# Another token order in the branch gates' products, with another block size in each of eight stages

## The chip, the cores and the metric

The kernel runs on one core of a Trainium2 chip. The metric is the time of one execution on the device in microseconds, as the median of several runs. TensorE multiplies and writes to the accumulator memory PSUM; ScalarE (ACT) and VectorE (DVE) work on tiles in SBUF and PSUM; SyncE (SP) and GpSimd (POOL) issue the transfers.

## The reference

One layer of a decoder trunk on 256 tokens of width 1024, in float32, every projection without a batch:

```python
proj = jnp.einsum("bsd,dn->bsn", x, w_in) + b_in
q_m, k_m, v_m, o_m, i_m, f_m, q_b, k_b, v_b, g_a, g_b = _split_cols(proj, SPLIT_SIZES)
# an mLSTM branch (4 heads x 256) gives y_a, an attention branch (8 heads x 128) gives y_b
merged = (jax.nn.sigmoid(g_a) * jnp.einsum("bsw,wd->bsd", y_a, w_branch_a)
          + jax.nn.sigmoid(g_b) * jnp.einsum("bsw,wd->bsd", y_b, w_branch_b))
mix = jnp.einsum("bsd,de->bse", merged, w_out)
x = layer_norm(ALPHA * x + mix, ln1_g, ln1_b)
# then a gated MLP with a short convolution, and a second layer norm
```

The change touches `g_a` and `g_b`, the two branch gates: each is a product of all 256 tokens with a 1024 x 1024 block of `w_in`, and a bias.

## The kernel before

All weights come from HBM as a stream of 89 chunks of 128 partitions x 2048 words (1 MB each), in the order that `chunk_order` gives. One chunk is one stage of the program. A chunk of a projection holds 256 output columns for all 1024 inputs, as 8 tiles (`KT`) of 128 inputs.

Every product is made of three float32r matmuls, so that nearly float32's precision is kept: each operand is split into a rounded high part (ScalarE, L93) and the remainder (VectorE, L94), and `mm3` (L126) adds high x high (L129), high weights x low tokens (L130) and low weights x high tokens (L131) into one PSUM tile.

In `mm_feat` (L133) the weights are the stationary operand, 128 columns of them, and the tokens are the moving one: all 256 columns of one input tile, `xh[:, k, :]`, 1024 contiguous bytes in each partition. One stage has two halves of 128 outputs (`j`), each with 8 input tiles and 3 matmuls: 48 matmuls of 256 columns. In `mm_tok` (L147) the roles are the other way round. While one matmul streams its columns, TensorE loads the next one's weights (the rows named PEld).

After four chunks for the output gate come four groups with eight stages each: `qm, qb, km, kb, vm, vb, ga, gb`. Two of these, `ga` and `gb`, are the branch gates (`step_gate`, L514). So there are eight gate stages, two in each group, each for 256 of the 1024 gate columns. A gate's PSUM tile is evacuated one stage later by two ScalarE instructions with the bias, which write the gate to `sg["ga"]` or `sg["gb"]` in SBUF. The gates are read much later, in the stages `wa` and `wb`, where the branches are merged.

The order of the work is written out by hand, stage by stage: in stage s the evacuation of stage s-1 and the split of chunk s+2 are issued, the load of chunk s+5, then the stage's matmuls, then what small products of the attention and the mLSTM fall into it (`side_pe`). The gate stages in groups 0 to 2 have such small products before and behind them: `psl` (attention logits, 256 columns and a float32 product of 128) and `psn` (258 columns). Three PSUM buffers (tag "mm") go round among the big stages.

Two functions set where in a buffer the weights of a chunk start: `shift` (L61) gives a number of columns by the kind of chunk, and `odd` (L1148) gives a few chunks 8 columns more or less in a part of the buffer and sets an input tile first.

Of the kernel before, what the change touches and what calls it, by code (L numbers as in the profile page):

```python
# [13 lines left out]
AF = mybir.ActivationFunctionType  # L14
# [4 lines left out]
P = 128  # L19
# [53 lines left out]
class Kernel:  # L73
# [26 lines left out]
    def split_parts(self, s):  # L100
        if s >= len(self.order) or s in self.w:
            return []
        raw = self.raw.pop(s)
        if s in self.extra:
            wh, wl = self.extra.pop(s)
            a = 8
        else:
            wh = self.stream.tile([P, WCOLS], F32R, tag="wh", name=f"wh{s}", bufs=3)
            wl = self.stream.tile([P, WCOLS], F32R, tag="wl", name=f"wl{s}", bufs=3)
            a = shift(*self.order[s])  # L110

        e, z, n, _ = odd(*self.order[s])
        wh, wl = (t[:, a - e:a + 2048 + z] for t in (wh, wl))
        edges = sorted({0, 256 if e else 0, 2048 if self.order[s][0] == "up" and self.order[s][1] >= 6 else 1024, 2048 - n, 2048})
        cuts = [(*(t[:, self.col(s, b):self.col(s, b) + d - b] for t in (wh, wl)), raw[:, b:d])
                for b, d in zip(edges, edges[1:])]
        self.w[s] = (wh, wl)
        return [lambda c=c: self.split_into(*c) for c in cuts]

    def col(self, s, c):  # L120

        e, z, n, _ = odd(*self.order[s])
        return c + (e if c >= 256 else 0) + (z if c >= 2048 - n else 0)
# [6 lines left out]
        mm(ps, ah, bl, start=False, stop=False)  # L130
        mm(ps, al, bh, start=False, stop=stop)  # L131

    def mm_feat(self, s, ps, xh, xl, mid=None):  # L133
        wh, wl = self.w.pop(s)
        _, _, n, first = odd(*self.order[s])
        ks = list(range(KT))

        for i, j in enumerate((1, 0) if first and n == P else (0, 1)):
            if i and mid:
                mid()  # L140
            js = ks[-1:] + ks[:-1] if first and 256 - n <= j * P else ks
            for k in js:
                a = self.col(s, k * 256 + j * P)
                self.mm3(ps[:, j, :], wh[:, a:a + P], wl[:, a:a + P], xh[:, k, :], xl[:, k, :], k == js[0],
                         k == js[-1])

    def mm_tok(self, s, ps, xh, xl, toks=(0, 1), kouter=False, ks=range(KT), first=None):  # L147
        todo = [(k, t) for k in ks for t in toks] if kouter else [(k, t) for t in toks for k in ks]
# [365 lines left out]
    def step_gate(self, s, n, g, voff):  # L514
        nc = self.nc
        ps = self.ps_main(f"ps_{n}{g}")
        self.mm_feat(s, ps, self.xth, self.xtl)

        def evac():
            for j in range(2):  # L520
                b = self.vec[:, voff + 2 * g + j:voff + 2 * g + j + 1]
                nc.scalar.activation(self.sg[n][:, 2 * g + j, :], ps[:, j, :], AF.Identity, bias=b)
        self.evac[s] = evac

    def step_ga(self, s, g, *a):
# [619 lines left out]
    Kernel(ctx, tc, *args).run()  # L1145


def odd(kind, i):  # L1148

    if kind == "kb":  # L1150
        return 0, 8, 128, False
    if kind == "ga" and i < NG - 1:
        return 0, 8, 128, True
    if (kind, i) == ("up", 2):
        return 0, 8, 256, True
    if (kind, i) in (("vb", 3), ("up", 0), ("up", 1)):
        return 8, 0, 0, False
    return 0, 0, 0, False
# [78 lines left out]
```

## Time and profile before

| | |
|---|---|
| median of three runs | 486.39 us (486.29 to 486.4) |
| the profiled execution | 486.21 us |
| its span, first to last instruction | 484.5 us |
| TensorE matmuls | 3832, busy 475.6 us |
| VectorE, ScalarE busy | 371.0 us, 286.8 us |
| TensorE clock granted, mean | 0.997 |
| ga and gb matmuls | 384 in eight stages, 64.8 to 226.2 us |
| ga and gb evacuations | 16 on ScalarE, 454 to 481 ns each |

A row of the time line has the start in microseconds from the span's start, the length, the engine, the line of the kernel, the operation, what it writes and reads, its shape, and how many equal ones are merged. The length of a matmul is modelled and holds its latency; matmuls overlap, so the time that one takes from the stream is the step from its start to the next one's start. A row of groups has the line, engine, operation, names, shapes and count, then busy microseconds and mean nanoseconds of one, then the idle time before it and what ended that.

### The profile page before, as it was taken

How to read it: one execution, taken by the hardware profiler on the slowest of the kernel's cores; microseconds unless marked ns; L12 is line 12 of the kernel's file. 1: busy time of each engine (PE TensorE's matmuls, PEld its weight loads, DVE VectorE, ACT ScalarE, POOL GpSimd, SP SyncE). 2: the span in 40 equal slices, each digit the busy share in tenths (PEclk: the TensorE clock that was granted, in tenths of full speed). 3: DMA queues.
4: the chain of work that ended last, by engine and by line, in shares of the span. 5: the costliest groups of instructions: out<-in, count | busy, mean ns of one | idle time of the engine just before them, and what ended most of it. 6: DMA issues, size and time to landing. Idle time of an engine off the chain costs nothing.

```text
span 484.5 us, 9391 instructions
## 1 busy us (share of the span) xinstructions
PE 475.6 (98%) x3832; PEld 459.9 (95%) x3832; DVE 371.0 (77%) x665; ACT 286.8 (59%) x483; POOL 27.2 (6%) x43
## 2 busy tenths in 40 slices
PE   8999999999999999999999999999999999999993
PEld 6999999999999999999999999999999999999983
DVE  4877986897689668985677798888668766776877
ACT  5568876686667666866654623766456544654530
POOL 0401011001100110002000001000000000000000
PEclk9999999999999999999999999999999999999998
DMA  7986676375536562653954581827454645455202
GB/s 219 317 296 176 227 256 202 113 274 187 212 110 251 193 211 95 239 200 113 389 195 173 180 342 61 287 89 261 175 218 163 224 179 189 175 216 202 88 1 87
DMA packets 20917, 94.28 MB, mean 195 GB/s; under 512 B 4837, under 2 KB 7793, under 8 KB 11017
## 3 DMA queue, kind: packets, MB, share of 16 engines
q1 hardware_dynamic: 16714, 87.61, 50.7%
q0 software_dynamic: 4160, 6.07, 3.9%
q8 instruction: 30, 0.49, 0.4%
q14 instruction: 13, 0.11, 0.1%
HBM read 92.58 MB, written 2.64 MB: 197 GB/s over the span
## 4 chain that ended last, share of the span: by engine, by line
PE 97%; DMA 1%; DVE 1%; SPq 0%; issue 0%; ACT 0%; DVEq 0%
PE ps_up L131 8%; PE ps_up L129 8%; PE ps_up L130 8%; PE ffn L131 4%; PE ffn L130 4%; PE ffn L129 4%; PE ps_qm L129 2%; PE ps_vb L131 2%; PE ps_vb L130 2%; PE ps_vb L129 2%; PE ps_ga L131 2%; PE ps_wb L131 2%; PE mix L131 2%; PE ps_qb L129 2%; PE ps_kb L131 2%; PE ps_wa L131 2%
## 5 line engine op out<-in xcount | busy, mean ns | idle before, releaser
L94 DVE TENSOR_TENSOR wl<-raw,wh 128x1024 fp32r<-128x1024 f32 (+5 forms) x147 | 180.3, 1264 | 30.6 <-ACT wh L93 28.0
L93 ACT CAST wh<-raw 128x1024 fp32r<-128x1024 f32 (+5 forms) x147 | 151.8, 1081 | 7.8 <-DMA raw<-in_wst_dram 4.4
L131 PE MATMUL ps_up<-x1h,wl 128*128 128x256 f32 x320 | 88.5, 276 | 0.0
L129 PE MATMUL ps_up<-x1h,wh 128*128 128x256 f32 x320 | 88.4, 276 | 0.0
L130 PE MATMUL ps_up<-x1l,wh 128*128 128x256 f32 x320 | 88.4, 276 | 0.0
L130 PEld LDWEIGHTS ps_up<-x1l,wh 128*128 128x128 f32 x320 | 60.1, 188 | 0.4
L129 PEld LDWEIGHTS ps_up<-x1h,wh 128*128 128x128 f32 x320 | 60.1, 188 | 0.3
L131 PEld LDWEIGHTS ps_up<-x1h,wl 128*128 128x128 f32 x320 | 60.1, 188 | 0.0
L1049 DVE SCALAR_TENSOR_TENSOR cu<-ps_up,vec,cu 128x255 f32<-128x255 f32 (+1 forms) x80 | 33.1, 476 | 20.3 <-ACT cu L1045 20.3
L93 ACT CAST hh<-cu 128x256 fp32r<-128x256 f32 x22 | 8.9, 407 | 46.8 <-DVE cu L1057 46.8
L131 PE MATMUL ffn<-wh,hl 128*128 128x512 f32 (+1 forms) x94 | 35.5, 378 | 0.0
L130 PE MATMUL ffn<-wl,hh 128*128 128x512 f32 (+1 forms) x94 | 35.5, 377 | 0.0
L129 PE MATMUL ffn<-wh,hh 128*128 128x512 f32 (+1 forms) x94 | 35.3, 375 | 0.0
L1045 ACT ACTIVATE cu<-ps_up,vec 128x256 f32<-128x256 f32 x40 | 16.7, 470 | 23.5 <-PE ps_up L131 23.5
L131 PEld LDWEIGHTS ffn<-wh,hl 128*128 128x128 f32 x94 | 17.7, 188 | 3.2
L130 PEld LDWEIGHTS ffn<-wl,hh 128*128 128x128 f32 x94 | 17.7, 188 | 3.1
L129 PEld LDWEIGHTS ffn<-wh,hh 128*128 128x128 f32 x94 | 17.7, 188 | 3.1
L129 PE MATMUL ps_qm<-xth,wh 128*128 128x256 f32 x64 | 18.1, 282 | 0.0
L129 PE MATMUL ps_ga<-xth,wh 128*128 128x256 f32 x64 | 18.0, 281 | 0.0
L129 PE MATMUL mix<-wh,mgh 128*128 128x256 f32 x64 | 17.8, 279 | 0.0
L129 PE MATMUL ps_vb<-wh,xth 128*128 128x256 f32 x64 | 17.8, 279 | 0.0
L129 PE MATMUL ps_qb<-xth,wh 128*128 128x256 f32 x64 | 17.8, 278 | 0.0
(319 smaller groups left out, 1439.5 us busy)
## 6 DMA issues: line engine op xcount, KB each, us to landing
raw<-in_wst_dram SPq DMA_DIRECT2D x77, 1024.0 KB, 4.9
raw<-in_wst_dram SPq DMA_DIRECT2D x8, 256.0 KB, 4.6
lnrow<-in_rows_dram POOLq DMA_DIRECT2D x4, 512.0 KB, 6.8
band<-table POOLq DMA_DIRECT2D x4, 384.0 KB, 12.9
xraw<-in_xt_dram SPq DMA_DIRECT2D x8, 128.0 KB, 4.0
toe<-band POOLq DMA_DIRECT2D x4, 256.0 KB, 3.6
xtok<-in_x_dram POOLq DMA_DIRECT2D x1, 1024.0 KB, 7.5
sgb<-in_wst_dram SPq DMA_DIRECT2D x4, 128.0 KB, 4.4
```

The costliest lines, as they stand in the source:

```text
L93: self.nc.scalar.copy(wh, raw)
L94: self.nc.vector.tensor_sub(wl, raw, wh.bitcast(F32))
L129: mm(ps, ah if first is None else first, bh, start=start, stop=False)
L130: mm(ps, ah, bl, start=False, stop=False)
L131: mm(ps, al, bh, start=False, stop=stop)
L1045: act.activation(cu[:, j, :], ps[:, j, :], AF.Copy, scale=tap(2, j))
L1049: v.scalar_tensor_tensor(cu[:, j, o:], ps[:, j, :S - o], tap(t, j), cu[:, j, o:], op0=ALU.mult, op1=ALU.add)
```

## The change

The tokens of a gate product are taken in another order. `token_order` gives, for each gate stage, three views: of the moving operand (`src`), of the PSUM tile where the product goes (`dst`), and of the place in SBUF to which the evacuation writes. `line(c)` is a walk in which the 256 tokens are taken in blocks of c from the two token halves in turn: c tokens from 0 on, c tokens from 128 on, the next c from c on, and so on. `out(...)` walks through contiguous words, only written with three dimensions; in the built program it is the plain contiguous pattern again.

| stage | moving read | PSUM write | evacuation reads PSUM | evacuation writes SBUF |
|---|---|---|---|---|
| ga 0 | blocks of 16 | contiguous | contiguous | blocks of 16 |
| gb 0 | blocks of 8 | contiguous | contiguous | blocks of 8 |
| ga 1 | blocks of 2 | contiguous | contiguous | blocks of 2 |
| gb 1 | blocks of 4 | contiguous | contiguous | blocks of 4 |
| ga 2 | blocks of 8 | blocks of 8 | blocks of 8 | blocks of 8 |
| gb 2 | blocks of 32 | contiguous | contiguous | blocks of 32 |
| ga 3 | contiguous | blocks of 16 | blocks of 16 | contiguous |
| gb 3 | blocks of 64 | contiguous | contiguous | blocks of 64 |

The gates end up in the same place and order as before. No instruction is added, removed or moved on any engine; the start addresses stay; the weights are read as before.

```diff
-    def mm_feat(self, s, ps, xh, xl, mid=None):
+    def mm_feat(self, s, ps, xh, xl, mid=None, way=None):
         wh, wl = self.w.pop(s)
+        src, dst, _ = way or (lambda t: t,) * 3
...
-                self.mm3(ps[:, j, :], wh[:, a:a + P], wl[:, a:a + P], xh[:, k, :], xl[:, k, :], k == js[0],
-                         k == js[-1])
+                self.mm3(dst(ps[:, j, :]), wh[:, a:a + P], wl[:, a:a + P], src(xh[:, k, :]), src(xl[:, k, :]),
+                         k == js[0], k == js[-1])
...
     def step_gate(self, s, n, g, voff):
         nc = self.nc
         ps = self.ps_main(f"ps_{n}{g}")
-        self.mm_feat(s, ps, self.xth, self.xtl)
+        way = token_order(n, g)
+        self.mm_feat(s, ps, self.xth, self.xtl, way=way)
...
-                nc.scalar.activation(self.sg[n][:, 2 * g + j, :], ps[:, j, :], AF.Identity, bias=b)
+                nc.scalar.activation(way[2](self.sg[n][:, 2 * g + j, :]), way[1](ps[:, j, :]), AF.Identity, bias=b)
...
+def token_order(n, g):
+
+    def line(c):
+        return lambda t: t.rearrange("p (j b c) -> p b j c", j=2, c=c)
+
+    def out(dims):
+        return lambda t: t.rearrange("p (a b c) -> p a b c", b=dims[1], c=dims[2])
+
+    return {
+        ("ga", 0): (line(16), out((8, 2, 16)), line(16)),
+        ("gb", 0): (line(8), out((16, 2, 8)), line(8)),
+        ("ga", 1): (line(2), out((64, 2, 2)), line(2)),
+        ("gb", 1): (line(4), out((32, 2, 4)), line(4)),
+        ("ga", 2): (line(8), line(8), line(8)),
+        ("gb", 2): (line(32), out((4, 2, 32)), line(32)),
+        ("ga", 3): (out((8, 2, 16)), line(16), out((8, 2, 16))),
+        ("gb", 3): (line(64), out((2, 2, 64)), line(64)),
+    }[n, g]
```

ScalarE's order around the evacuation of ga 1 shows it: what follows is the row of before, and then that of the change. The shape at a row's end is that of what is written.

```order
L660 CAST sph1_1533<-wt1_1517 128x384
L93 CAST wh20_1515<-raw20_1323 128x1024 x2
L759 ACTIVATE lg3_1614,sm3_1616<-lg3_1614,mx3_1615 128x128
L759 ACTIVATE lg3_1614,sm3_1616<-lg3_1614,mx3_1615 128x256
L522 ACTIVATE sga_100<-ps_ga1_1547,vec_95 128x256 x2
L93 CAST wh21_1612<-raw21_1389 128x1024 x2
```

```order
L662 CAST sph1_1533<-wt1_1517 128x384
L93 CAST wh20_1515<-raw20_1323 128x1024 x2
L761 ACTIVATE lg3_1614,sm3_1616<-lg3_1614,mx3_1615 128x128
L761 ACTIVATE lg3_1614,sm3_1616<-lg3_1614,mx3_1615 128x256
L524 ACTIVATE sga_100<-ps_ga1_1547,vec_95 128x64x2x2 x2
L93 CAST wh21_1612<-raw21_1389 128x1024 x2
```

Nothing moved: the same instructions stand in the same order (two lines further down in the file), and the two evacuations write 64 x 2 runs of 2 words instead of one run of 256. A product's moving operand changes in the same way.

## The prediction

> **What bounds the kernel now.** I read the page's busy shares first, then its chain of waits, then the time line of TensorE stage by stage.
>
> ```profile
> PE 475.6 (98%) x3832; PEld 459.9 (95%) x3832; DVE 371.0 (77%) x665; ACT 286.8 (59%) x483; POOL 27.2 (6%) x43
> PEclk9999999999999999999999999999999999999998
> PE 97%; DMA 1%; DVE 1%; SPq 0%; issue 0%; ACT 0%; DVEq 0%
> ```
>
> TensorE is 97% of the chain that ended last, at the full granted clock from end to end. So a nanosecond added to a matmul is a nanosecond of the run, and one on ScalarE is free until a matmul waits for it. A busy share says nothing of the rate, because matmuls overlap. The rate is the step from one start to the next. Here is a whole stage, the second product of the first branch: its first row, its last, and the first row of the next stage.
>
> ```profile
> 233.36 0.28 PE L129 MATMUL ps_wb<-ybh,wh 128*128 128x256 f32 x1
> ...
> 238.68 0.28 PE L131 MATMUL ps_wb<-ybh,wl 128*128 128x256 f32 x1
> 238.80 0.28 PE L129 MATMUL ps_wa<-yah,wh 128*128 128x256 f32 x1
> ```
>
> 48 matmuls take 5.44 us, or 113.3 ns each. That is the fast step for 256 moving columns. The gate stages are near it: the first runs from 64.75 to 70.31.
>
> ```profile
> 64.75 0.36 PE L129 MATMUL ps_ga<-xth,wh 128*128 128x256 f32 x1
> ...
> 70.31 0.28 PE L129 MATMUL psl<-kbh,qbh 128*128 128x256 f32 x1
> ```
>
> That is 5.56 us for 48; its first steps come behind a float32 product and are slow. But the fast step is not the only one. These are two stages of one kind, the values of groups 1 and 3, with the same count, shape and lines:
>
> ```profile
> 107.08 0.28 PE L129 MATMUL ps_vb<-wh,xth 128*128 128x256 f32 x1
> ...
> 112.52 0.28 PE L129 MATMUL pss<-qmh,kmh 128*128 128x256 f32 x1
> ```
>
> ```profile
> 207.53 0.28 PE L130 MATMUL ps_vb<-wl,xth 128*128 128x256 f32 x1
> ...
> 213.07 0.28 PE L129 MATMUL psl<-kbh,qbh 128*128 128x256 f32 x1
> ```
>
> The first takes 5.44 us for 48 (113.3 ns), the second 5.54 us for 47 (117.9 ns), without a wait in it. In the code they differ in what comes before and in where the first columns of the weights lie (the function odd moves them by 8). A third family, the last products of the second MLP weight, gives the price once more, next to a step of twice the columns:
>
> ```profile
> 463.72 0.39 PE L129 MATMUL ffn<-wh,hh 128*128 128x512 f32 x1
> ...
> 472.56 0.28 PE L129 MATMUL ffn<-wh,hh 128*128 128x256 f32 x1
> ...
> 476.75 0.28 PE L131 MATMUL ffn<-wh,hl 128*128 128x256 f32 x1
> ```
>
> 39 steps of 512 columns take 8.84 us, 226.7 ns each, twice 113.3. Then 35 steps of 256 columns take 4.19 us, 119.7 ns each. So contiguous products of one shape run at 113 or at 118 to 120 ns, and which of the two depends on how the two streams that TensorE reads at once, the moving columns and the next weights, lie to each other. That the cause is this relation is my reading of the rows; the two prices are measured.
>
> **The change part by part.** No instruction is added, removed or moved: 384 matmuls (eight stages of 48) and 16 evacuations get other access patterns. I take three terms.
>
> *Term 1, the order of the moving reads.* In seven stages a matmul reads blocks of 16, 8, 2, 4, 8, 32 and 64 tokens from two places 512 bytes apart (336 matmuls). Blocks of 64 are so long that the stream looks contiguous for most of the time: I take 0 for that stage, at most the phase price below. In the other stages the moving stream advances through two places at half speed each, while the weights are read as before, so a relation tuned for the contiguous order is lost. I price that loss by the row nearest in shape, 119.7 ns against 113.3: 6.4 ns. For the five stages with blocks of 4, 8, 16 and 32 that is 5 x 48 x 6.4 ns = 1.54 us. The low end is 0 (the stage keeps 113.3).
>
> *Term 2, the stage with blocks of 2* (ga of group 1). It visits 128 places for 256 columns, eight bytes at each. No row has such a read. The low end is the phase price, 6.4 ns a matmul, 0.31 us. The high end is that each visit takes the time of twice the columns, the 512-column step: 226.7 - 113.3 = 113.4 ns, 5.44 us. The row nearest in columns and bytes is the low one, but the number of visits is that of a long read; I take the geometric middle, 27 ns, 1.29 us.
>
> [...]
>
> *Term 3, the writes and the evacuation.* Two stages write PSUM in blocks (ga of group 2 in blocks of 8, ga of group 3 in blocks of 16); the latter reads contiguously. I take 0, since each block is at least 8 neighbouring words; the other end is a rival below. On ScalarE the evacuations read or write blocks. The nearest rows are casts of 64, 256 and 512 elements; the first writes blocks of 8:
>
> ```profile
> L93 ACT CAST wh<-wif 128x64 fp32r<-128x64 f32 x1 | 0.2, 244 | 0.2 <-DMA wif<-in_wif_dram 0.2
> L93 ACT CAST wh<-sgb 128x256 fp32r<-128x256 f32 x4 | 1.6, 404 | 0.2 <-DMA sgb<-in_wst_dram 0.2
> L93 ACT CAST wh<-sgb 128x512 fp32r<-128x512 f32 x2 | 1.2, 622 | 0.4 <-DMA sgb<-in_wst_dram 0.3
> ```
>
> 256 elements more cost 218 ns, 0.85 ns each; the line through the two long casts gives 404 - 192 x 0.85 = 240 ns for 64, and the cast into blocks of 8 took 244. So blocks of 8 cost nothing on ScalarE. For shorter blocks the bound is the element part once more, 0.22 us an instruction. Even that is hidden:
>
> ```profile
> 75.33 0.82 ACT L522 ACTIVATE sga<-ps_ga,vec 128x256 f32<-128x256 f32 x2
> 76.05 1.99 ACT L93 CAST wh<-raw 128x1024 fp32r<-128x1024 f32 x2
> ...
> 77.39 2.36 DVE L94 TENSOR_TENSOR wl<-raw,wh 128x1024 fp32r<-128x1024 f32 x2
> ...
> 85.27 0.28 PE L129 MATMUL ps_qb<-xth,wh 128*128 128x256 f32 x1
> ```
>
> Behind the pair in ScalarE's queue stands the cast of the weights of the stage that starts at 85.27, and behind that VectorE's remainder, done at 79.75; the same stage takes over the PSUM buffer. More than 5 us of cover stand against 0.44 us. Without that cover it would cost 0.44 us in each of the two stages with blocks under 8.
>
> *A later stage.* A disturbed start can spoil a whole stage (the 117.9 ns of group 3). A spoiled neighbour costs 4.6 x 48 = 0.22 us, seven at most 1.5 us; float32 products and transposes stand between most of them, so I take 0.
>
> *The sum.* 1.54 + 1.29 = 2.83 us on the profiled execution's 486.21 (span 484.5 and 1.7 around it) gives 489.0; the median of the runs lies 0.18 above that execution, so **489.2 us**.
>
> **The rivals.**
>
> *A. The phase is lost and the smallest block pays something* (my forecast). For it: 113.3, 117.9 and 119.7 in products of one shape. Against it: the slow ones are rare in this kernel, and nothing shows that a stream in two places is among them. 488.2 to 491 us.
>
> *B. Nothing happens.* The reads keep 113.3 whatever their order from blocks of 2 up, or the patterns are merged into plain ones. For it: 512 columns take exactly twice the time of 256, so the step follows the column count alone where the streams agree. 486.4 us.
>
> *C. The price goes by visits.* From the point where a visit brings fewer than four words, it takes a slot of its own: the stage with blocks of 2 doubles, 1.54 + 5.44 = 6.98 us, 493.4 us. For it: 113.3 ns for 1 KB a partition may already be all that the port gives. Against it: nothing in the trace shows a read limit apart from the column count.
>
> *D. Broken PSUM writes, or broken patterns as such, halve the rate.* Writes alone: two stages x 48 x 113.4 ns = 10.9 us, 497.3 us, or 500.1 us with the forecast. In rows it has no support: every product here writes contiguous columns.
> [...]
>
> *E. Faster.* If some of the 113.3 ns is itself a clash of the two streams, reading two places in turn may avoid it. The shortest full step in the trace is that of the eight transposes:
>
> ```profile
> 309.28 1.03 PE L1017 MATMUL ps_upT<-ident,tu 128*128 128x128 f32 x8
> 310.07 0.36 PE L129 MATMUL ps_up<-x1h,wh 128*128 128x256 f32 x1
> ```
>
> Eight steps take 0.79 us, 99 ns each. The most that seven stages could win by it is 336 x 14 ns = 4.8 us, 481.6 us. That step is of another kind (half the columns), and no 256-column stage here is under 113; a third of it, 484.8 us, would be much.
>
> **How the numbers follow.** A 0.45, B 0.19, C 0.17, D 0.07, E 0.09, and 0.03 for spoiled neighbours on top of A. What can be told from no change is 0.2%, 0.97 us, so faster is E (0.09), same is B (0.19), slower is the rest (0.72). The forecast is that of A, 489.2 us. The range 486.0 to 493.8 us takes in B, A and C with the bounds of term 2, and leaves out D and E. A alone would be 488.2 to 491 us.
>
> **What would show it.** In the profile after, the step within each gate stage: 113.3 ns with blocks of 64 and where only the write is broken, about 120 with blocks of 4 to 32, and 120 to 227 with blocks of 2. Stages that do not change should keep 113.3. The evacuations should stay at 0.46 to 0.48 us, those with blocks of 2 and 4 under 0.7, and no matmul should wait for them. I am wrong if the stages with long blocks (16, 32) are as slow as the one with 2, if the contiguous read with a broken write is slow, or if any gate stage steps under 113.

## The result: 491.27 us, 1.0% slower

The changed kernel takes 491.27 us (median of 3 runs, 490.82 to 491.52) against 486.39: 1.0100 times the time before, with a 95% interval of 1.0077 to 1.0123. The profiled execution is 491.27 us (span 489.6), 5.06 us more than that of before. The forecast was 2.8 us.

The page of the kernel after, its busy shares, granted clock and chain of waits:

```profile
PE 479.2 (98%) x3832; PEld 463.6 (95%) x3832; DVE 371.1 (76%) x665; ACT 287.0 (59%) x483; POOL 28.0 (6%) x43
PEclk9999999999999999999999999999999999999998
PE 97%; DMA 1%; DVE 1%; SPq 0%; issue 0%; ACT 0%; DVEq 0%
```

TensorE is still 97% of the chain, at a granted clock of 0.996 in the mean. Behind the opening it waits for nothing, as before; its matmuls take longer. (In the opening it waits 1.6 us for its first weights in place of 0.2, but the products ahead of that wait end sooner, and the next one starts only 0.12 us later than before.) The time line of TensorE has it stage by stage: the first product of a gate stage and the first row behind it, for blocks of 2 (from 115.08), of 4 (from 124.87), a contiguous read with a write in blocks of 16 (from 219.75) and blocks of 64 (from 225.79).

```profile
115.08 0.41 PE L129 MATMUL ps_ga<-xth,wh 128*128 128x256 f32 x1
...
116.14 0.34 PE L129 MATMUL ps_ga<-xth,wh 128*128 128x256 f32 x1
116.31 0.34 PE L130 MATMUL ps_ga<-xtl,wh 128*128 128x256 f32 x1
116.48 0.34 PE L131 MATMUL ps_ga<-xth,wl 128*128 128x256 f32 x1
...
123.20 0.29 PE L129 MATMUL psl<-kbh,qbh 128*128 128x256 f32 x1
...
124.87 0.29 PE L129 MATMUL ps_gb<-xth,wh 128*128 128x256 f32 x1
...
130.97 0.82 PE L772 MATMUL pst<-ident,lg 128*128 128x128 f32 x6
...
219.75 0.28 PE L129 MATMUL ps_ga<-xth,wh 128*128 128x256 f32 x1
...
225.22 0.82 PE L772 MATMUL pst<-ident,lg 128*128 128x128 f32 x6
225.79 0.37 PE L129 MATMUL ps_gb<-xth,wh 128*128 128x256 f32 x1
...
231.33 0.60 PE L723 MATMUL psy<-ident,yt 128*128 128x128 f32 x4
```

48 products take 8.12 us with blocks of 2, 6.10 with blocks of 4, and 5.47 and 5.54 in the last two. In the middle of the first stage the products start every 0.17 us, evenly: no wait stands out, each product is slower. All eight stages, from such rows of both traces (the step is the mean inside the stage, without its first three products and its last):

| stage | read, write | before, us | after, us | more, us | step after, ns |
|---|---|---|---|---|---|
| ga 0 | blocks of 16 | 5.56 | 5.84 | 0.28 | 120.0 |
| gb 0 | blocks of 8 | 5.46 | 5.77 | 0.31 | 120.0 |
| ga 1 | blocks of 2 | 5.56 | 8.12 | 2.56 | 168 |
| gb 1 | blocks of 4 | 5.46 | 6.10 | 0.64 | 127 |
| ga 2 | blocks of 8, PSUM written in 8 | 5.56 | 6.00 | 0.44 | 123.3 |
| gb 2 | blocks of 32 | 5.46 | 5.71 | 0.25 | 118.8 |
| ga 3 | contiguous, PSUM written in 16 | 5.46 | 5.46 | 0 | 113.3 |
| gb 3 | blocks of 64 | 5.54 | 5.54 | 0 | 113.3 |

That is 4.48 us of the 5.06. The rest is in stages that the change doesn't touch. The clearest is the stage vb of group 0, which runs ahead of every changed product; here is its first product and the row behind it, of before and then of after:

```profile
57.12 0.28 PE L129 MATMUL ps_vb<-wh,xth 128*128 128x256 f32 x1
...
62.65 0.41 PE L603 MATMUL ps_gc<-ident,gates 4*128 4x4 f32 x4
```

```profile
57.31 0.28 PE L129 MATMUL ps_vb<-wh,xth 128*128 128x256 f32 x1
...
63.08 0.41 PE L605 MATMUL ps_gc<-ident,gates 4*128 4x4 f32 x4
```

5.53 us before, 5.77 after, for the same instructions in the same order. Here only the first two products are late: they take 0.23 and 0.22 us, and the others step at 113.6 ns. qm 2 and the fourth up stage take 0.20 us more each, with every product slower (117.7 ns). The opening gives 0.19 us more up to the first qm stage. Other stages gain: the small products behind ga 0 take 0.13 us less, and the second up stage, slow in the kernel before, 0.16 us less.

ScalarE's evacuations, the groups of after:

```profile
L524 ACT ACTIVATE sgb<-ps_gb,vec 128x256 f32<-128x256 f32 x8 | 3.4, 476 | 0.2 <-PE ps_gb L131 0.2
L524 ACT ACTIVATE sga<-ps_ga,vec 128x256 f32<-128x256 f32 x8 | 3.3, 467 | 0.0
```

476 and 467 ns on average, against 477 and 463 before. The pair that writes blocks of 2 took 476 and 480 ns, against 455 and 462; none of the other fourteen, with blocks of 4 and up or a contiguous write, moved by more than 3 ns.

### The profile page after: what moved, and what is told of

The parts are those of the page before. It is cut to its first block, busy times and chain, and to the rows that moved or that the text cites. A ratio compares the mean times of both kernels' runs of the same rounds, so it can differ in the third digit from the quotient of the medians.

```text
span 489.6 us, 9391 instructions
## 1 busy us (share of the span) xinstructions
PE 479.2 (98%) x3832; PEld 463.6 (95%) x3832; DVE 371.1 (76%) x665; ACT 287.0 (59%) x483; POOL 28.0 (6%) x43
## 4 chain that ended last, share of the span: by engine, by line
PE 97%; DMA 1%; DVE 1%; SPq 0%; issue 0%; ACT 0%; DVEq 0%
PE ps_up L131 8%; PE ps_up L129 8%; PE ps_up L130 8%; PE ffn L131 4%; PE ffn L130 4%; PE ffn L129 4%; PE ps_ga L131 2%; PE ps_ga L129 2%; PE ps_ga L130 2%; PE ps_gb L130 2%; PE ps_gb L129 2%; PE ps_gb L131 2%; PE ps_qm L129 2%; PE ps_vb L130 2%; PE ps_vb L129 2%; PE ps_qm L130 1%
## 5 line engine op out<-in xcount | busy, mean ns | idle before, releaser
L129 PE MATMUL ps_ga<-xth,wh 128*128 128x256 f32 x64 | 19.2, 300 | 0.0
L131 PE MATMUL ps_ga<-xth,wl 128*128 128x256 f32 x64 | 19.0, 297 | 0.0
L130 PE MATMUL ps_ga<-xtl,wh 128*128 128x256 f32 x64 | 19.0, 297 | 0.0
L129 PE MATMUL ps_gb<-xth,wh 128*128 128x256 f32 x64 | 18.2, 285 | 0.0
L130 PE MATMUL ps_gb<-xtl,wh 128*128 128x256 f32 x64 | 18.1, 283 | 0.0
```

Source lines behind the costliest of these rows:

```text
L129: mm(ps, ah if first is None else first, bh, start=start, stop=False)
```

## The experiments

The runs change the walk through the tokens stage by stage, and some of them also where the weights of the gate stages start; the rest of the kernel stays. So each run holds up to eight measurements. The edits are shown shortened. A step is the mean start-to-start time of a product inside a stage. The letters of theories in the expectations are theirs, not those of the prediction's rivals. A total without an interval is a single time; there the steps carry the argument.

**Without the two smallest blocks.** The blocks of 2 and 4 become 64.

```diff
-        ("ga", 1): (line(2), out((64, 2, 2)), line(2)),
-        ("gb", 1): (line(4), out((32, 2, 4)), line(4)),
+        ("ga", 1): (line(64), out((2, 2, 64)), line(64)),
+        ("gb", 1): (line(64), out((2, 2, 64)), line(64)),
```

> The change with its two smallest blocks (2 and 4 tokens, both stages of group 1) replaced by blocks of 64. Theory S (a cost where the moving read and the read of the next weights meet; about 6 ns a matmul for walks of 8 to 32, none for 64): the two stages go back to 5.56 and 5.46 us, together 3.2 us less than in the change, and the run lies near 488 us. Theory V (each visit to a block costs on its own): the same saving of 3.2 us, since 64 is 4 visits a matmul. If the run falls by clearly less than 3 us, the two stages' length was not what the change cost.

487.96 us (6 runs), 1.0034 times before (1.0022 to 1.0047). Both stages are back at 113.3 to 113.6 ns, and the others stay as in the changed kernel. So of the 4.9 us about 3.3 come from these two stages, and the three-dimensional form of the pattern alone costs nothing.

**All eight stages with blocks of 64.**

```diff
-    return {...}[n, g]
+    return line(64), out((2, 2, 64)), line(64)
```

> All eight gate stages read in blocks of 64. Theory S: a block of 64 tokens is 256 bytes, and the stream looks as in the contiguous order: every stage at 113.3 ns a matmul, the run at the time of before within 0.5 us. Theory V: 4 visits a matmul instead of 1; by the line through 16 visits for 5.8 ns, about 1 ns a matmul, 384 x 1 = 0.4 us more. A plain price for any pattern of three dimensions would show here as more than 1 us.

486.41 us, 1.0001 times before (0.9992 to 1.0011), every stage at 113.3 to 113.7 ns. Two places 512 bytes apart are free here, where the stream stays 256 bytes at each.

**Blocks of 16 against eight starts of the weights.** My reading of the price was that the walk loses a relation between the moving columns and the next weights. If so, the price must depend on where the weights start. All eight gate stages read in blocks of 16, and their weights start at word 0, 8, 16 and so on to 56 of a buffer, without the further shift and the order of input tiles that `odd` gives to ga.

```diff
+GATE_SHIFT = {("ga", 0): 0, ("gb", 0): 8, ("ga", 1): 16, ("gb", 1): 24, ("ga", 2): 32, ("gb", 2): 40, ("ga", 3): 48, ("gb", 3): 56}
 def shift(kind, i):
+    if (kind, i) in GATE_SHIFT:
+        return GATE_SHIFT[kind, i]
...
-    if kind == "ga" and i < NG - 1:
-        return 0, 8, 128, True
```

> All eight gate stages read in blocks of 16, and each stage has its weights at another offset: 0, 8, 16, 24, 32, 40, 48, 56 words into the buffer (16 in the change). Theory S: the step depends on the offset and differs between the stages by 5 ns or more, and some offset gives the fast 113.3 ns back. Theory V: the weights have no part in it, so all eight stages step at 119 to 121 ns.

489.59 us. The step is 120.0 ns at seven starts and 121.2 at word 24. First product and next row of the stages with start 0 and start 56 (from 65.07, and from 223.32), on TensorE's time line:

```profile
65.07 0.36 PE L134 MATMUL ps_ga<-xth,wh 128*128 128x256 f32 x1
...
70.91 0.28 PE L134 MATMUL psl<-kbh,qbh 128*128 128x256 f32 x1
...
223.32 0.37 PE L134 MATMUL ps_gb<-xth,wh 128*128 128x256 f32 x1
...
229.17 0.60 PE L728 MATMUL psy<-ident,yt 128*128 128x128 f32 x4
```

5.84 and 5.85 us. My reading falls: over these eight starts the price of blocks of 16 moves by 1.2 ns at most.

**The contiguous read against the same eight starts.** Here the steps do differ.

```diff
-        ("ga", 0): (line(16), out((8, 2, 16)), line(16)),
+        ("ga", 0): (flat, flat, flat),     # and so in all eight stages, flat = the pattern as it is
```

> All eight gate stages read contiguously, with the same eight offsets of the weights (0, 8, 16, 24, 32, 40, 48, 56 words). Theory S: only 16 words (as before) is sure to give 113.3 ns; others cost 5 to 10 ns a matmul, as the stages of before with 117.9 and 119.7 ns do. Theory V: 113.3 ns at all eight, since the read is one visit.

490.98 us, 4.8 us more than before, with contiguous reads throughout. The steps at starts 0 to 56 are 120.0, 118.3, 117.8, 118.7, 118.7, 120.0, 117.8 and 116.7 ns. That the start sets them is not shown: each start stands in one stage only, and at word 16, which gives 117.8 here, the gb stages of the kernel before step at 113.3. After the last of them, eight stages wa and wb and the four of the output projection, which nothing in this run changes, stay slow. The first three of them, on TensorE's time line:

```profile
229.91 0.28 PE L134 MATMUL ps_wa<-yah,wh 128*128 128x256 f32 x1
...
235.56 0.28 PE L134 MATMUL ps_wb<-ybh,wh 128*128 128x256 f32 x1
...
241.22 0.28 PE L134 MATMUL ps_wa<-yah,wh 128*128 128x256 f32 x1
...
246.87 0.28 PE L134 MATMUL ps_wb<-ybh,wh 128*128 128x256 f32 x1
```

5.65 us each against the 5.44 of before: 117.8 ns in place of 113.3. So the contiguous stream ran at a second, lower rate here, and it held from one stage to the next. That is the 118 to 120 ns from which I took the price of the walk. The walk of 16 is not simply this rate: in six of the eight stages it is 1.3 to 3.3 ns slower than the contiguous read at the same start, and in two it is equal.

**Only the writes in blocks.** Contiguous reads, PSUM written in blocks of 16, 8, 2, 4, 2 (in two sweeps over every other pair), 8, 32 and 64.

```diff
-        ("ga", 1): (line(2), out((64, 2, 2)), line(2)),
+        ("ga", 1): (out((64, 2, 2)), line(2), out((64, 2, 2))),     # and so on: the read is contiguous, the write is not
```

> Contiguous reads in all eight gate stages; only the PSUM writes go in blocks, of 16, 8, 2, 4, 2 in two sweeps 16 bytes apart, 8, 32, 64. The change had a write in blocks of 16 at 113.8 ns, as before. Theory S and theory V both say that writes cost nothing: 113.3 ns (115.8 with the slow start in the ga stages) everywhere, and the time of before within 0.5 us. [...]

486.65 us, beside 486.14 for the kernel before on the same chip. Every gate stage steps at 113.3 to 113.6 ns, those of blocks of 2 too. Here is the first of these, with the row behind it:

```profile
114.42 0.36 PE L129 MATMUL ps_ga<-xth,wh 128*128 128x256 f32 x1
...
119.98 0.28 PE L129 MATMUL psl<-kbh,qbh 128*128 128x256 f32 x1
```

5.56 us, as before. The 0.5 us is not theirs: against the profiled execution of before, TensorE is 0.37 us behind ahead of all gate stages, and the fourth up stage is 0.20 us slower, as in the changed kernel; small products give 0.13 back.

**Blocks of 2 against the starts of the weights.** As with 16, now `line(2)` in all eight stages.

```diff
-        ('ga', 0): (line(16, 2), lambda t: t.rearrange("p (b j c) -> p b j c", j=2, c=16), line(16, 2)),
+        ('ga', 0): (line(2, 2), lambda t: t.rearrange("p (b j c) -> p b j c", j=2, c=2), line(2, 2)),
```

> All eight gate stages read in blocks of 2, with the weights at 0, 8, 16, 24, 32, 40, 48, 56 words. The change had 168 ns a matmul for blocks of 2 at 16 words. Theory S: the step differs between the offsets by 10 ns or more. Theory V: 168 ns within 3 at all eight, because 128 visits cost what they cost; the run then is 486.4 + 384 x 55 ns = 507.5 us.

508.37 us. The steps are 166.6, 166.8, 168.1, 169.8, 173.3, 170.0, 173.3 and 173.3 ns: a little by start, but 53 to 60 above the plain step everywhere.

**More places, and sweeps.** `line(c, j)` reads blocks of c from j places in turn. All weights of the gate stages start at word 16, without the shift of `odd`.

The entry is the walk of the read.

```diff
+        ("ga", 0): line(16, 4)    # 4 places, 256 bytes apart
+        ("gb", 0): line(4, 4)
+        ("ga", 1): line(2, 4)
+        ("gb", 1): line(2, 64)    # the first half of every 16 bytes, then the second half of each
+        ("ga", 2): line(4, 32)    # every other 16 bytes, then the rest
+        ("gb", 2): line(1, 128)   # every other word, then the rest
+        ("ga", 3): line(4, 16)    # 16 places, 64 bytes apart
+        ("gb", 3): line(16, 8)    # 8 places, 128 bytes apart
```

> Walks of other geometry, the weights at 16 words in all stages. In order of the stages: four places 256 bytes apart in blocks of 16, of 4 and of 2; one sweep over the first half of every 16-byte piece and a second over the other (blocks of 2, 64 neighbours apart by 16 bytes); two sweeps in blocks of 4 (32 bytes apart); two sweeps over every second word; sixteen places 64 bytes apart in blocks of 4; eight places 128 bytes apart in blocks of 16. Theory V: the step follows the block alone: 120 for blocks of 16, 127 for 4, 168 for 2, more than 168 for single words. Theory S with a memory that repeats at some distance: the distance between the places counts, so that blocks of 4 differ by more than 10 ns between places 32, 64 and 256 bytes apart, and a sweep that only goes forward (the two-sweep walks) costs less than one that jumps back and forth.

505.47 us. In that order: 119.9, 138.8, 226.6, 229.3, 117.7, 229.8, 114.3 and 121.3 ns. Two of these decide: the sweep over half of every 16 bytes (from 128.13) and over every other 16 bytes whole (from 175.78).

```profile
128.13 0.39 PE L129 MATMUL ps_gb<-xth,wh 128*128 128x256 f32 x1
...
139.11 0.85 PE L772 MATMUL pst<-ident,lg 128*128 128x128 f32 x6
...
175.78 0.36 PE L129 MATMUL ps_ga<-xth,wh 128*128 128x256 f32 x1
...
181.52 0.28 PE L129 MATMUL psl<-kbh,qbh 128*128 128x256 f32 x1
```

10.98 against 5.74 us. Skipping whole groups of 16 bytes and taking them later leaves the step at 117.7 ns; taking half of each and coming back for the other half doubles it, 229.3 ns. Every other word, with the rest taken later, makes twice the visits to as many groups and takes about the same, 229.8 ns. So the time of these three sweeps goes with how often they come to a group of 16 bytes: 64 times in 117.7 ns, 128 times in 229.3 and 229.8. Counted in units of 8 bytes the first would not have doubled, and in units of 32 the second would have. Nor does the length of the blocks alone set the price, as theory V has it: blocks of 4 cost 1.0 ns from sixteen places, 13.4 from two and 25.5 from four.

**Twice the columns.** Is the price paid once per product, or per column? The gate stages stream 512 columns (two input tiles) into one PSUM tile.

```diff
-                self.mm3(dst(ps[:, j, :]), wh[:, a:a + P], wl[:, a:a + P], src(xh[:, k, :]), src(xl[:, k, :]), ...)
+                self.mm3(ps.rearrange("p k s -> p (k s)"), wh[:, a:a + P], wl[:, a:a + P], src(two[0]), src(two[1]), ...)
```

> The gate products multiply 512 moving columns (two input tiles side by side) instead of 256, so the gates are not the reference's; one load of weights now goes with twice the columns. The walks: contiguous, blocks of 8, of 2, of 4, of 16, of 32, contiguous, blocks of 64, over two places 1 KB apart. Contiguous should step at 226.7 ns. Theory S (cost where the weight load meets the read, once a matmul): the extra is that of 256 columns: 53 ns for blocks of 2, 13 for 4, 6 for 8 to 32, so 280, 240, 233. Theory V (cost by visit): the extra doubles: 106, 27, 12, so 333, 253, 239.

539.03 us. The contiguous stages step at 233.3 ns in this run, so they run at the lower rate, and blocks of 64, 32, 16, 8, 4 and 2 at 233.3, 236.7, 240.0, 243.3, 252.3 and 327.3. The base was disturbed, so the run was made again with all weights at start 0:

```diff
+GATE_SHIFT = {("ga", 0): 0, ("gb", 0): 0, ...}
```

> 512 moving columns as in e8_wide (gates not the reference's), the weights at offset 0, where the last products of the MLP step at 226.7 ns. Walks: contiguous, blocks of 8, 2, 4, 16, 32, contiguous, 64, over two places 1 KB apart. Theory V (the walk itself pays, by columns): the plain step is 226.7 and the extras are twice those of 256 columns: 240 for blocks of 8 and 16, 253 for 4, 327 for 2, 238 for 32. Theory S (the read meets the weight load, once a matmul): extras as for 256 columns, 233 for 8 and 16, 240 for 4, 280 for 2.

540.1 us. The contiguous stages and blocks of 64 step at 226.7 ns, as 512 columns do elsewhere in the kernel; blocks of 32, 16, 8, 4 and 2 at 236.7, 240.0, 243.3, 250.0 and 328.3. Blocks of 2 (from 125.97) and a contiguous stage (from 255.51):

```profile
125.97 0.57 PE L134 MATMUL ps_ga<-xth,wh 128*128 128x512 f32 x1
...
141.79 0.29 PE L134 MATMUL psl<-kbh,qbh 128*128 128x256 f32 x1
...
255.51 0.40 PE L134 MATMUL ps_ga<-xth,wh 128*128 128x512 f32 x1
...
266.42 0.82 PE L782 MATMUL pst<-ident,lg 128*128 128x128 f32 x6
```

Over the contiguous step that is 10, 13.3, 16.6, 23 and 101 ns more. For 256 columns it is 5.5, 6.7, 6.7, 13.4 and 53. Twice the columns pay about twice the price (1.7 to 2.5 times), so it goes with the columns and is not paid once per product. And the walks of 32, 16 and 8 stand at the same 236.7, 240.0 and 243.3 in both runs, whether the contiguous stages are at 233.3 or at 226.7: the lower rate is not added to theirs.

**Other distances.** Two places 512 bytes apart might hit the same part of the memory. Blocks of 4 at 512, 528, 544, 576, 640 and 768 bytes, blocks of 2 at 528 and 576.

```diff
+                    c, d, q = way[0], way[1], min(k, KT - 2) * 256
+                    two = [t.rearrange("p k s -> p (k s)")[:, q:q + 2 * d].rearrange("p (j r) -> p j r", j=2)
+                           [:, :, 0:P].rearrange("p j (b c) -> p b j c", c=c) for t in (xh, xl)]
```

> Blocks of 4 from two places whose distance is 512, 528, 544, 576, 640 and 768 bytes, then blocks of 2 from places 528 and 576 bytes apart (the second place lies in the next input tile in part, so the gates are not the reference's). At 512 bytes the change had 127 ns for 4 and 168 for 2. Theory B (fetches that follow each other clash when their addresses lie a multiple of 256 bytes apart; blocks of 4 fetch no more lines than the contiguous read): 127 at 512 and 768 bytes, 113 to 115 at 528 to 640. Theory V (a price by visit): 127 at all six. Blocks of 2: by B between 113 and 168, nearer to 113 if a line just left is still at hand; by V 168.

496.89 us. Blocks of 4: 126.8, 127.9, 123.7, 122.0, 126.7 and 126.9 ns; blocks of 2: 166.2 and 166.7. The distance moves the price of blocks of 4, 13.4 ns, by 6 at most, and 528 bytes are as slow as 512; it is no clash of 512 bytes. As in the run on contiguous starts, the stages wa and wb took 5.65 us each here, and in the one before this too.

**Fewer groups of 16 bytes, and single words.** If coming to a group sets the rate, reading the same words again should be faster, and a walk with twice the visits should tell whether a visit costs by itself. The other four stages read each 16 bytes twice (gb 0), one group of 16 bytes 64 times (ga 1), each word four times (ga 2) and pairs twice (ga 3).

```diff
+        ('ga', 0): (lambda t: t[:, 0:128].unsqueeze(2).to_broadcast([P, 128, 2]), ...),   # each word twice
+        ('gb', 1): (lambda t: t.rearrange("p (j b) -> p b j", j=2), ...),                 # single words from the two halves
+        ('gb', 2): (lambda t: t[:, 0:64].unsqueeze(1).to_broadcast([P, 4, 64]), ...),     # 64 words four times
+        ('gb', 3): (flat, flat, flat),                                                    # contiguous
```

> 256 moving columns out of fewer addresses, so all gates but the two named last are not the reference's (tokens are repeated). In order: each of 128 words twice; each 16-byte line of 32 twice; one line 64 times; single words from the two halves in turn; each of 64 words four times; a piece of 64 words four times over; each pair of 64 words pairs twice; and, with nothing changed, the contiguous read. Theory L (the contiguous read is itself bound by lines: 64 lines of 16 bytes at 1.77 ns are the 113.3 ns, a line that is fetched anew costs this, a word of the line in hand nothing): the walks that stay in a line for 8 or 16 words fall below 111 ns; the piece of 64 words four times stays at 113 (64 fetches). Theory C (113.3 ns is what 256 columns cost, by whatever address): 113.3 ns for all of them. Single words from two halves: 256 visits; L with a memory of the last two lines 113 to 170, without one 4 x 113 = 453 ns.

486.04 us, 486.56 for the kernel before beside it. Repeated words, pairs and groups step at 111.7 ns, 64 words four times at 113.3, and the single words at 111.7. The contiguous stage ran at the lower rate, 117.8, with nothing changed in it against the kernel before, where it steps at 113.3; so something else than the start of the weights can tip it too. (64 words four times come to a group as often as the contiguous read, and take as long as its better rate.) Single words (from 120.90), then contiguous (from 220.17):

```profile
120.90 0.27 PE L129 MATMUL ps_gb<-xth,wh 128*128 128x256 f32 x1
...
126.26 0.82 PE L772 MATMUL pst<-ident,lg 128*128 128x128 f32 x6
...
220.17 0.36 PE L129 MATMUL ps_gb<-xth,wh 128*128 128x256 f32 x1
...
225.92 0.60 PE L723 MATMUL psy<-ident,yt 128*128 128x128 f32 x4
```

5.36 us with 256 visits to two places, where 128 visits with pairs took 8.12 in the changed kernel. So a visit has no price of its own here, and the time does not grow with their number: among the blocks from two places the pairs are the slowest. And 113.3 ns is not the floor of 256 columns, though nothing here went more than 1.6 ns under it: one group of 16 bytes read 64 times takes 111.7 too.

**A version that reads single words.** Gates, qm and km, wa and wb, and 20 up stages read the tokens as single words from two places in turn, 2112 products. The evacuations put the order right, or write the tokens so that the walk yields them in order.

```diff
+def halves(t):
+    return t.rearrange("p (j b) -> p b j", j=2)
+def walk(t):
+    return t.rearrange("p (t j b) -> p t b j", t=2, j=2)
...
-        self.mm_feat(s, ps, self.xth, self.xtl)
+        self.mm_feat(s, ps, self.xth, self.xtl, src=halves, dst=even)
...
-        self.mm_feat(s, ps, self.x1h, self.x1l, self.back if i == 2 else None)
+        self.mm_feat(s, ps, self.x1h, self.x1l, self.back if i == 2 else None, src=walk, dst=plain)
```

> An attempt at a version faster than both kernels. The moving side of the gate stages, of the four stages that make qm and km, of the eight stages wa0 to wb3 and of the up stages from the third on reads single words from two places in turn (halves 512 bytes apart; in the up stages 256 bytes apart). Where the engine that evacuates reorders anyway, it stores the tokens so that the order comes out as before; the gates and qm, km are put in order at their evacuation. All products are done. Theory V as it now stands (two streams of whole lines, word by word in turn, are the fastest reading: 111.7 ns a product in the run with single words): 111.7 in place of 113.3, 1.67 ns on about 384 + 384 + 384 + 960 products, 3.5 us, so 482 to 483.5 us, if the rearranged stores of the evacuations stay hidden. Rival: 111.7 came from the distance of 512 bytes or from the gates' place alone, and the up stages at 256 bytes stay at 113.3 or slow down: then 484 to 486. Second rival: the rearranged stores take longer and their waits stand in the chain, or plain stages beside them go to 117.8 and eat it: 486 to 489.

484.05 us (5 runs, 483.61 to 484.66), 0.9951 times before (0.9937 to 0.9965): 2.3 us less than the kernel before and 7.2 less than the changed one, though above the 482 to 483.5 that I had expected. Two gate stages on TensorE's time line, from 162.58 and from 213.46, then the split of the layer's middle into its two parts among the groups, and what TensorE waits for between 220 and 330 us:

```profile
162.58 0.36 PE L129 MATMUL ps_ga<-xth,wh 128*128 128x256 f32 x1
...
168.02 0.28 PE L129 MATMUL psl<-kbh,qbh 128*128 128x256 f32 x1
...
213.46 0.27 PE L129 MATMUL ps_ga<-xth,wh 128*128 128x256 f32 x1
...
218.82 0.82 PE L772 MATMUL pst<-ident,lg 128*128 128x128 f32 x6
```

```profile
L988 DVE TENSOR_TENSOR x1l<-ps_t,x1h 128x512 fp32r<-128x512 f32 x4 | 4.5, 1124 | 1.1 <-ACT x1h L987 1.0
L987 ACT CAST x1h<-ps_t 128x512 fp32r<-128x512 f32 x4 | 4.4, 1095 | 14.1 <-PE ps_t L979 14.1
```

```profile
PE ps_up L131 <- DVE x1l L988: 0.5, 1, 0.5
```

The walked stages step at 111.7 ns, those of the up stages with their places 256 bytes apart too, and 2112 x 1.67 ns makes 3.5 us. The matmuls' steps got 2.6 us shorter in all, as the span did. What was given back stands around the split. It now writes word by word into two places, and takes 1095 and 1124 ns; before it took 588 and 688:

```profile
L94 DVE TENSOR_TENSOR x1l<-ps_t,x1h 128x512 fp32r<-128x512 f32 x4 | 2.8, 688 | 1.2 <-ACT x1h L93 1.2
L93 ACT CAST x1h<-ps_t 128x512 fp32r<-128x512 f32 x4 | 2.4, 588 | 15.1 <-PE ps_t L976 15.1
```

TensorE waits for it once, 0.5 us, where before there was no such wait. The first two up stages, with the transposes in them, are 0.75 and 0.31 us longer; the first wa stage is 0.16 us longer. The evacuations of gates got slower as well (699 and 727 ns in place of 463 and 477), and nothing waited for those.

## Why the prediction was right in sign and short in size

**Side and range** came from the right place: TensorE is the whole chain, and the walk made its products slower. 491.27 lies inside the range, 2.1 us above the forecast and a little above the forecast's own upper end of 491. Of the 2.2 us that the forecast was short of the profiled 5.06, 1.27 lie in term 2, 0.38 in term 1 and 0.58 in the stages that I put at nothing.

**Term 1** (blocks of 4 to 32, 1.54 us) measured 1.92 us. The price of 6.4 ns was met by blocks of 16 and 8 (6.7) and nearly by 32 (5.5). Blocks of 4 pay 13.4, twice as much, and the stage that also writes PSUM in blocks of 8 steps 3.3 ns above its like. Writes alone are free (113.3 to 113.6 ns), so that is the pair of them or something else in that stage; no run separated it.

**Term 2** (blocks of 2, 1.29 us) is the step that failed in size: 2.56 us, 53 ns a product and not 27. Its bounds held (6.4 and 113.4). I leaned to the low one by the geometric middle because the low row was nearest in columns and bytes; the measured price is just under the arithmetic middle, 60. Nor do pairs have one price: a product of them takes 168 ns from two places, 227 from four and 229 in a sweep.

**Term 3** (writes and evacuations, 0) was right: 113.3 ns with PSUM written in blocks, evacuations 467 and 476 ns, no wait. That the blocks have at least 8 neighbouring words, from which I took the 0, was not needed: the run that only writes is at 113.3 to 113.6 ns down to blocks of 2. It refutes rival D with its halved rate.

**A later stage** (0) was 0.58 us. I had looked for stages behind the changed ones; vb 0 and the opening ran ahead of them all. In every run but the one with blocks of 64 throughout and the last one, some of these plain stages took 0.2 us more than before, and not always the same ones; in several the second up stage took 0.16 us less. What tips a stage into the lower rate stays open; shown is only that it can last from stage to stage, as the 117.8 ns of the twelve stages in the run on contiguous starts.

**The cause** that I gave, the lost relation to the next weights, was wrong; that its price was nearly right was luck. Eight starts of the weights left the walk at 120.0 to 121.2, while the contiguous read in the same eight stages took 116.7 to 120.0, and with 512 columns the walks kept their steps when the contiguous stages changed theirs. So I read the walk and the lower rate as two effects of nearly the same size. What they may share, no run shows.

**The rivals.** C (a price by visits, a doubled stage) was right that the smallest block pays far more; but 53 ns is half of its price, and single words, with twice the visits, pay nothing. No run shows a slot that begins below four words a visit: blocks of 4 pay 13.4 ns already. E was right that reading two places in turn can lift part of the 113.3 ns, to 111.7, but only with single words, which the change doesn't use; whether that part is a clash of the two streams, no run shows. Its bound took the 99 ns of the transposes for the shortest step of the trace, which it is not: two float32 products of 128 columns (psl, from 70.66 to 70.80) take 70 ns each. Steps of half the columns bound nothing here. B fell in six stages and held in the two with blocks of 64 and with the write alone.

**What stays open.** Coming to each group of 16 bytes twice, for half its words each time, makes the read twice as slow (229 ns). But how often a walk comes to a group doesn't explain the 111.7: single words from two places need as many groups as the contiguous read if each is taken once, and one group read 64 times is no faster than they are. Nor does any run show why blocks of 4 to 32 pay 5 to 13 ns, and why pairs take 168 ns from two places and 227 from four.

## What to carry to other kernels

Where TensorE is the whole chain, the order of the moving operand is worth a run of its own: for the float32r products here, pairs from two places take half again as long (168 ns against 113.3), blocks of 64 words cost nothing (113.3), and single words from two places are 1.4% faster than contiguous ones (111.7). Put an order right on the side that has cover: here writes to PSUM in blocks of 2 to 64 were free under a contiguous read (113.3 to 113.6 ns), and ScalarE's evacuations could be slowed without harm (699 and 727 ns in place of 463 and 477, with no wait for them), while about a quarter of the gain was given back (3.5 us less the 2.6 that remained), most of it around a store between two dependent stages. Before you take a price for an effect from rows that merely look alike, vary what you believe to be its cause: the walk kept its 120 ns when its supposed cause was varied, and the rows that gave the price were of another kind.

## What was not expected of the hardware

- Contiguous products of 256 columns run at 113.3 ns or at a lower steady rate, mostly 117.8 and up to 120, without a wait in either; the granted clock was 1.00 in the vb stage of group 1 (113.3) and in that of group 3 (117.8). In three runs eight unchanged stages or more stayed at 117.8 from start to end.
- The step of 113.3 ns was beaten by other reads: 111.7 with single words from two places 512 or 256 bytes apart, and with words read twice.
- The price did not fall steadily with the length of the blocks. From two places 512 bytes apart it is minus 1.6 ns at single words, 53 at pairs, 13.4 at 4, 6.7 at 8 and 16, 5.5 at 32 and none at 64.
- Products that write PSUM in blocks of 2 in two places kept the contiguous read's step, 113.3 to 113.6 ns.
